# A looping load queue with register rows, and three outputs moved off TensorE in the last macro tile but one of rot90

## The chip, the cores and the metric

The kernel runs on one core of one Trainium2 chip. The metric is the time of one execution on the device, in microseconds (us). One execution per version is also taken with the hardware profiler; its trace gives the views used here.

## The reference

`x` is 8192 x 8192, float32. The kernel computes

```python
def reference(x, k):          # k = 1
    return np.rot90(x, k)
```

so `out[i, j] = x[j, 8191 - i]`: 268 MB are read, 268 MB are written, and nothing is calculated. Every 128x128 block has to be transposed on the way.

## The kernel before

**Tiles.** The input is cut into 16 macro tiles of 1024 rows x 4096 columns (numbered `kk`, 0 to 15). A macro tile is loaded in eight loads of 128 rows (2 MB each, row block `t`) and leaves in eight outputs (2 MB each, `j`), every output being 512 input columns of all 1024 rows. Load number `m` is `kk * 8 + t`, output number `n` is `kk * 8 + j`.

**Memory.** Loads land in two buffers in turn (`LAND = 2`; the first loads also use others). VectorE (DVE) takes each landed load and puts it, with its columns reversed, into the `ring`, which holds one macro tile less one chunk. An output is assembled in one of three buffers (`OUTS = 3`, chosen by the list `TURN`, L38) and stored from there. At the very end the landing buffers serve as output buffers too. Load `m` takes the ring places that output `m - 8` leaves, so DVE can only turn load `m` once output `m - 8` has been read out of the ring.

**Two ways to transpose.** `by_pe` (L196) says which outputs TensorE makes: all eight of tiles 0 and 15, outputs 0 and 4 of tiles 1 to 13, and outputs 0, 2, 4, 6, 7 of tile 14. For these DVE copies the load's columns into the ring (COPY), TensorE transposes 32 blocks of 128x128 against the identity into PSUM (`ps`), and ScalarE (ACT) evicts them into the output buffer. For all other outputs ("moved" ones) DVE transposes 32x32 squares on the way into the ring (STREAM_TRANSPOSE), and the squares then only need to be copied to their places in the output buffer: 16 copies of 32 partitions x 1024 elements, of which DVE makes 3, GpSimd (POOL) 8 and ACT 5 (`BY_DVE`, `BY_POOL`). One corner chunk of each tile has no place in the ring and goes through TensorE in any case; that is why output 7 has copies of 896 elements.

**Order of the work around the change.** Each engine has one program in order, and they meet in semaphores:

- SyncE (SP) issues nearly all loads (`by_sync`, L446, from load 5 on; `load_in_turn`, L400); ACT issues loads 1, 3 and 5 and halves of loads 6 to 9. Load `m` waits until DVE has turned the load that was in its buffer before (`taken`, L307).
- DVE (`by_vector`, L450), for load `m`: makes its 3 copies of output `n = m - 8` if that one is moved (after `room_for`, L295, has seen the store out of its buffer landed), waits for the load, waits until POOL and its own copies of output `n` are through (or TensorE has read it), and then turns load `m` into the ring, in the pieces that `by_pe` and the reach of one instruction give.
- POOL (`by_gpsimd`, L421) makes its 8 copies of each moved output; the eighth waits for ACT's five.
- ACT (`by_scalar`, L539) goes through the outputs in order: evictions for TensorE's, five copies for moved ones, and then it issues the store. For a moved output it waits first until DVE's first piece of load `n + 8` is done, which stands for POOL and DVE being through.
- TensorE (`by_tensor`, L493) transposes its outputs in order, in two PSUM halves.

**Loops.** An engine's program is recorded first (`Program`, L109) and then played. Two macro tiles make one turn of a loop on the engine (`loop`, L136); wait values are worked out from the loop register. In the kernel before, POOL loops over tiles 1 to 12, DVE and TensorE over tiles 2 to 13, in 6 turns each; SP and ACT are written out in full. All played instructions are issued on one line, L104, so the profile tells them apart by their tiles. SP's loads, which are not played, stand on L391.

The lines that decide who makes what, and the loops:

```python
    def by_pe(kk):
        if kk in (0, KK - 1):
            return list(range(J))
        return BY_PE if kk < KK - 2 else [*range(0, J, 2), J - 1]
```

Of the kernel before, what the change touches and what calls it, by code (L numbers as in the profile page):

```python
# [6 lines left out]
P = 128  # L7
# [3 lines left out]
T = R // P  # L11
W = 4096
# [48 lines left out]
class Place:  # L61


    def __init__(self, out, top, rows, left, cols):
        self.out, self.top, self.rows, self.left, self.cols = out, top, rows, left, cols
# [8 lines left out]
        return (self.top, self.rows, self.cols)  # L74


def key_of(v):
    if isinstance(v, bass.AP):
        return (v.tensor.name, v.offset, str(list(v.ap)))
    if isinstance(v, Place):  # L80
        return v.key()
    return str(v)


class Op:
# [13 lines left out]
    def run(self, e, shift=0, value=None):  # L99
        if self.name == "wait_ge":  # L100
            e.wait_ge(self.args[0], self.args[1] if value is None else value)  # L101
            return
        kwargs = {k: v.at(shift) if isinstance(v, Place) else v for k, v in self.kwargs.items()}
        i = getattr(e, self.name)(*self.args, **kwargs)  # L104
        if self.inc:
            i.then_inc(*self.inc)


class Program:  # L109
# [26 lines left out]
    def loop(self, nc, e, first, times):  # L136
        turns = [
            [op for kk in (first + 2 * i, first + 2 * i + 1) for op in self.parts[kk]]
            for i in range(times)
        ]  # L140
        for i, ops in enumerate(turns):
            assert len(ops) == len(turns[0]), (str(e.engine), i, len(ops), len(turns[0]))
            for a, b in zip(ops, turns[0]):
                assert a.key() == b.key(), (str(e.engine), i, a.key(), b.key())
        with nc.Fori(1, times + 1, engines=[e.engine]) as i:  # L145
            passed = nc.alloc_semaphore("passed") if e is nc.gpsimd else None
            waited = False
            for ops in zip(*turns):
                op = ops[0]
                if waited and op.name != "wait_ge" and passed is not None:  # L150
                    e.sem_inc(passed, 1)  # L151
                waited = op.name == "wait_ge"
                if op.name == "wait_ge":
                    n = [o.args[1] for o in ops]
                    step = n[1] - n[0]
                    assert n == [n[0] + k * step for k in range(times)]
                    assert n[0] > 0 and step >= 0
                    op.run(e, value=i * step + (n[0] - step) if step else n[0])
                    continue
                left = [v.left for o in ops for v in o.kwargs.values() if isinstance(v, Place)]  # L160
                if left:
                    step = left[1] - left[0]
                    assert left == [left[0] + k * step for k in range(times)]
                    op.run(e, shift=i * step - step)
                else:
                    op.run(e)
# [7 lines left out]
def kernel(tc: tile.TileContext, x: bass.AP, k: bass.AP, out: bass.AP):  # L174
# [21 lines left out]
    def by_pe(kk):  # L196
        if kk in (0, KK - 1):
            return list(range(J))
        return BY_PE if kk < KK - 2 else [*range(0, J, 2), J - 1]

    def in_quadrants(kk, j):
        return j not in by_pe(kk)
# [145 lines left out]
    def at(v, first, dims):  # L348
        return bass.AP(
            tensor=v.tensor, offset=v[:, first : first + 1].offset, ap=[v.ap[0], *dims]  # L350
        )
# [32 lines left out]
    def load(e, m, queue):  # L384
        r0, c0 = macros[m // T]
        b = load_buf(m)
        rows = slice(0, P)
        if m in BOTH:
            rows = slice(0 if queue is nc.sync else 1, P, 2)
        r = r0 + m % T * P  # L390
        e.dma_start(  # L391
            out=bufs[b][rows, :], in_=x[r : r + P, c0 : c0 + W][rows, :]
        ).then_inc(s_land[b], 16)

    def queues(m):
# [4 lines left out]
    def load_in_turn(e, m, queue):  # L400
        if queue not in queues(m):
            return
        last = [i for i in range(m) if load_buf(i) == load_buf(m)]
        taken(e.wait_ge, last[-1])
        load(e, m, queue)
# [4 lines left out]
    def turned_in(n):  # L410
        kk, _, (j,), _ = outs[n]
        return rev[kk * T + T - 1 - (j == J - 1), j]

    with tc.tile_critical():
        for m in range(LAND + OUTS):
            for e in queues(m):
                load(e, m, e)
    tc.close()
    tc.compile()  # L419

# [24 lines left out]

    def by_sync(e):  # L446
        for m in range(LAND + OUTS, n_load):
            load_in_turn(e, m, nc.sync)

    def by_vector(e):  # L450
        wait = once(e)
        for m in range(n_load):
            kk, t = divmod(m, T)
            e.part(kk)
            b = load_buf(m)
            n = m - T
            if n >= 0 and moved[n]:
                room_for(wait, n)
                wait(s_rev, turned_in(n))
                for to, of in moves(n, pairs[:BY_DVE]):  # L460
                    i = e.tensor_copy(out=to, in_=of)
                i.then_inc(s_dve, 1)
            e.wait_ge(s_land[b], landings(m))
            if n >= 0:
                if moved[n]:
                    e.wait_ge(s_pool, moved_until(n))
                    e.wait_ge(s_dve, moved_until(n))
                else:
                    e.wait_ge(s_half, turned_until(n))
            for js in pieces[m]:  # L470
                if (m, js[0]) == (n_load - 1, J - 1):
                    e.wait_ge(s_half, turned_until(KK * J - J))
                if kk < KK - 1 and (t, js[0]) == (T - 1, J - 1):
                    wait(s_rev, rev[m, 0])
                    e.tensor_copy(
                        out=at(bufs[b][:], 0, [[CH, 1], [1, CH]]), in_=landed(b, js)
                    ).then_inc(s_rev, 1)
                    continue
                turn = e.transpose if in_quadrants(kk, js[0]) else e.tensor_copy
                turn(out=chunk(kk, t, js), in_=landed(b, js)).then_inc(s_rev, 1)  # L480
# [12 lines left out]
    def by_tensor(e):  # L493
        e.part(-1)
        wait = once(e)
        e.wait_ge(s_id, 2)
        used = {}
        for n, some in in_turn():
            kk, ts, js, blocks = outs[n]
            e.part(kk)  # L500
            rows = len(ts) * P
            order = [(part, f) for part in some for f in part[2]]
            if js[0] == 0 and kk < KK - 1:
                late = parts[n][-1]
                order.sort(key=lambda o: (o[0] == late, o[1] % rows, o[1]))
            last = dict(order)
            for part, f in order:
                _, h, cols = part
                j, off = blocks[f // rows]
                t = ts[f % rows // P]  # L510
                if kk < KK - 1 and js[0] == 0 and f == parts[n][-1][2][0]:
                    m = kk * T + T - 1
                    wait(s_rev, rev[m, J - 1])
                    wait(s_freed, kk)
                    for g in range(G):
                        i = e.transpose(
                            corner[:, g * P : g * P + P],
                            bufs[load_buf(m)][:, g * P : g * P + P],
                            ident,
                        )  # L520
                    i.then_inc(s_corner, 1)
                if n == KK * J - J and h:
                    wait(s_freed, KK - 1)
                if used.get(h, part) != part:
                    wait(s_ev, evicted[used[h][0]] + 1)
                wait(s_rev, rev[kk * T + t, j])
                if part == parts[n][0] and f == last[part] and n != FIRST[1] and not tight(n):
                    room_for(wait, n)
                to = cols.index(f) * P
                i = e.transpose(  # L530
                    ps[h][:, to : to + P],
                    chunk(kk, t, [j])[:, 0, off : off + P],
                    ident,
                )
                if f == last[part]:
                    i.then_inc(s_half, 1)
                    used[h] = part
# [46 lines left out]
                in_=bufs[b][:, : groups * rows].rearrange("m (g f) -> m g f", f=rows),  # L584
            ).then_inc(s_store[b], 16)

    by_sync(nc.sync)
    for e, by, first, times in (
        (nc.gpsimd, by_gpsimd, 1, 6),
        (nc.vector, by_vector, 2, 6),  # L590
        (nc.tensor, by_tensor, 2, 6),
        (nc.scalar, by_scalar, None, 0),
    ):
        program = Program()
        by(program)
        program.play(nc, e, first, times)
# [39 lines left out]
```

## Time and profile before

| | |
|---|---|
| time, median of 3 runs | 1258.96 us (1258.8 to 1259.03) |
| the profiled execution: its own time | 1259.08 us |
| the profiled execution: span from first to last instruction | 1257.8 us |
| HBM read and written | 268.44 MB and 268.44 MB, 427 GB/s over the span |
| busy share of the span: PE, DVE, ACT, POOL | 24%, 63%, 48%, 59% |
| instructions | 6012 |
| loads | 124 of 2 MB and 8 halves of 1 MB; 125 of them issued by SP, 7 by ACT |
| stores | 128 of 2 MB, all issued by ACT |

How to read it: the span is cut into 40 slices of about 31 us for the rows of busy tenths; the DMA row there is the mean busy share of the core's 16 DMA engines, and the GB/s row what they moved. A timeline row has the start in us from the beginning of the span, the duration, the engine, the line, the operation, the tiles written and read, the shapes, and how many instructions were merged; in square brackets stands the idle time before it and what ended it. `ACTq` is ScalarE's sequencer, which issues DMAs. The chain of waits is the chain of work that ended last, in order of time. The packet records are the single DMA transfers in the trace: each 2 MB load or store is 128 packets of 16 KB, eight on each of the 16 DMA engines, and loads and stores have a queue each.

### The profile page before, as it was taken

What the parts mean: (1) busy time and instruction counts of PE and PEld (TensorE: products, weight loads), DVE (VectorE), ACT (ScalarE), POOL (GpSimd) and SP (SyncE); (2) the same over time, 40 slices, a digit from 0 to 9 for tenths busy, and PEclk for the clock granted to TensorE, in tenths of its full rate; (3) what the DMA queues carried; (4) which work ended last, traced back from release to release, by engine and by line L of the source; (5) the groups of instructions that cost most, each with busy time, mean ns of one, the idle gap of its engine ahead of it and who ended that gap; (6) DMA issues with size and microseconds to landing.
All of it is one profiled execution on the core that took longest, in us unless ns stands there. A gap on an engine that the chain in (4) does not pass through costs nothing.

```text
span 1257.8 us, 6012 instructions
## 1 busy us (share of the span) xinstructions
PE 302.9 (24%) x1556; PEld 264.8 (21%) x1556; DVE 793.8 (63%) x535; ACT 599.6 (48%) x556; POOL 744.0 (59%) x654
## 2 busy tenths in 40 slices
PE   1555013130131301313022130221302213024273
PEld 0454012130121301212012120121202212024273
DVE  2544866668666676666867667676677766764410
ACT  0334364463644636446364453645535455355364
POOL 0001966668666686666956668576685766965500
PEclk9987556555555555555556555565555556555597
DMA  9999999999999999999999999999999999999999
GB/s 400 420 430 429 429 429 429 429 431 430 430 430 429 430 428 430 428 430 430 430 430 429 431 428 431 428 430 428 430 430 429 430 429 431 427 423 428 427 428 381
DMA packets 36946, 537.09 MB, mean 427 GB/s; under 512 B 4160, under 2 KB 4160, under 8 KB 4160
## 3 DMA queue, kind: packets, MB, share of 16 engines
q10 hardware_dynamic: 19184, 278.93, 52.2%
q1 hardware_dynamic: 17744, 257.96, 48.0%
q8 instruction: 7, 0.11, 0.0%
q14 instruction: 11, 0.09, 0.0%
HBM read 268.44 MB, written 268.44 MB: 427 GB/s over the span
## 4 chain that ended last, share of the span: by engine, by line
DMA 71%; DVE 14%; ACT 4%; POOL 4%; issue 3%; PE 2%; ACTq 0%; DVEq 0%; SPq 0%; POOLq 0%
DMA buf<-in_x_dram 57%; DMA out_dram<-buf 14%; DVE ring L104 14%; ACT buf L104 4%; POOL buf L104 4%; PE ps L104 2%; ACTq L104 0%; DVE buf L104 0%; DVEq L101 0%; SPq L391 0%; DVEq L145 0%; POOLq L101 0%; SPq L311 0%; POOLq L151 0%; SPq L419 0%
## 5 line engine op out<-in xcount | busy, mean ns | idle before, releaser
L104 POOL COPY buf<-ring 32x1024 f32<-32x1024 f32 (+1 forms) x648 | 743.3, 1147 | 440.4 <-DMA out_dram<-buf 244.2
L104 ACT COPY buf<-ring 32x1024 f32<-32x1024 f32 (+1 forms) x405 | 414.8, 1024 | 324.2 <-DVE ring L104 292.5
L104 PE MATMUL ps<-head,ring 128*128 128x128 f32 x1496 | 290.7, 372 | 889.4 <-ACT buf L104 535.8
L104 PEld LDWEIGHTS ps<-head,ring 128*128 128x128 f32 x1496 | 255.3, 197 | 921.5 <-ACT buf L104 548.7
L104 DVE COPY ring<-buf 128x1024 f32<-128x1024 f32 (+5 forms) x152 | 157.7, 1044 | 415.6 <-DMA buf<-in_x_dram 320.1
L104 DVE STREAM_TRANSPOSE ring<-buf 128x3072 f32<-128x3072 f32 (+2 forms) x125 | 358.0, 2872 | 0.0
L104 ACT COPY buf<-ps 128x2048 f32<-128x2048 f32 (+4 forms) x149 | 183.3, 1278 | 313.6 <-DMA out_dram<-buf 149.3
L104 DVE COPY buf<-ring 32x1024 f32<-32x1024 f32 (+1 forms) x243 | 289.5, 1192 | 2.2
L104 PE MATMUL ps<-head,buf 128*128 128x128 f32 x60 | 15.2, 401 | 46.3 <-DVE buf L104 46.3
L104 PEld LDWEIGHTS ps<-head,buf 128*128 128x128 f32 x60 | 9.7, 199 | 52.0 <-issue 44.6
L104 DVE COPY buf<-buf 128x512 f32<-128x512 f32 x15 | 5.8, 387 | 0.0
L104 ACT ACT_TABLE_LOAD x1 | 1.3, 1283 | 3.4 <-PEq L419 3.4
L104 POOL MEMSET head<- 128x128 f32 x1 | 0.2, 204 | 2.9 <-POOLq L419 2.9
L104 POOL TENSOR_SCALAR_AFFINE_SELECT head<-head 128x128 f32<-128x128 f32 x1 | 0.3, 293 | 0.2 <-POOL head L104 0.2
L617 POOL MEMSET const-float32-0.0<- 128x1 f32 x1 | 0.1, 98 | 0.2 <-issue 0.2
L104 ACT COPY head<-head 128x1 f32<-128x1 f32 x1 | 0.2, 191 | 0.0
L617 POOL MEMSET const-bfloat16-1.0<- 128x1 bf16 x1 | 0.1, 100 | 0.0
L617 POOL MEMSET const-uint8-127<- 128x1 uint8 x1 | 0.1, 100 | 0.0
L617 POOL MEMSET const-float32-1.0<- 128x1 f32 x1 | 0.1, 98 | 0.0
## 6 DMA issues: line engine op xcount, KB each, us to landing
out_dram<-buf ACTq DMA_DIRECT2D x128, 2048.0 KB, 15.8
buf<-in_x_dram SPq DMA_DIRECT2D x121, 2048.0 KB, 15.0
buf<-in_x_dram ACTq DMA_DIRECT2D x3, 2048.0 KB, 16.9
buf<-in_x_dram SPq DMA_DIRECT2D x4, 1024.0 KB, 16.1
buf<-in_x_dram ACTq DMA_DIRECT2D x4, 1024.0 KB, 16.4
```

The lines of the kernel that those rows point to most:

```text
L104: i = getattr(e, self.name)(*self.args, **kwargs)
L617: nc = _bacc.Bacc("TRN2", target_bir_lowering=False, num_devices=1)
```

## The change

Four things change.

1. SP's program is recorded and played like the others: loads of tiles 2 to 13 are issued in a loop of 6 turns. The input rows are given by a new class `Rows`, which adds the loop register to the first row. In the loop each wait stands as an instruction of its own in front of the load and also counts up a semaphore; behind it come two small register instructions (the wait's value, the address) for every load. The destination and the length of the loads are unchanged, 128 rows of 4096 columns.
2. `by_pe` gives tile 14 the outputs 0 and 4 like tiles 1 to 13. Outputs 2, 6 and 7 of tile 14 become moved ones: 24 copies more on POOL, 15 on ACT in place of its evictions, 9 on DVE; and DVE turns the loads of tile 14 with one smaller COPY and one larger STREAM_TRANSPOSE each.
3. TensorE loops over tiles 1 to 14 and POOL over tiles 1 to 14, in 7 turns; TensorE starts its list of waits anew at tile 1, so that the turns are alike.
4. DVE waits, before its copies of a moved output, for the turn of the last of the tile's moved outputs instead of that output's own; at that point it has already gone through all of the tile's loads itself.

```diff
+class Rows:
+    def __init__(self, x, top, few, cols):
+        self.x, self.left, self.few, self.cols = x, top, few, cols
+
+    def at(self, shift):
+        if isinstance(shift, int):
+            return self.x[self.left + shift : self.left + shift + P, self.cols][self.few, :]
+        return self.x[bass.ds(self.left + shift, P), self.cols]
...
         with nc.Fori(1, times + 1, engines=[e.engine]) as i:
-            passed = nc.alloc_semaphore("passed") if e is nc.gpsimd else None
+            passed = None
+            if e in (nc.gpsimd, nc.sync):
+                passed = nc.alloc_semaphore(f"passed_{e.engine}")
...
                     op.run(e, value=i * step + (n[0] - step) if step else n[0])
+                    if e is nc.sync:
+                        e.sem_inc(passed, 1)
+                        waited = False
                     continue
...
     def by_pe(kk):
         if kk in (0, KK - 1):
             return list(range(J))
-        return BY_PE if kk < KK - 2 else [*range(0, J, 2), J - 1]
+        return BY_PE
...
         e.dma_start(
-            out=bufs[b][rows, :], in_=x[r : r + P, c0 : c0 + W][rows, :]
+            out=bufs[b][rows, :], in_=Rows(x, r, rows, slice(c0, c0 + W))
         ).then_inc(s_land[b], 16)
...
     def by_sync(e):
         for m in range(LAND + OUTS, n_load):
+            e.part(m // T)
             load_in_turn(e, m, nc.sync)
...
-                wait(s_rev, turned_in(n))
+                wait(s_rev, max(turned_in(i) for i in range(n - n % J, n - n % J + J) if moved[i]))
...
             e.part(kk)
+            if n == J:
+                wait = once(e)
...
-    by_sync(nc.sync)
     for e, by, first, times in (
-        (nc.gpsimd, by_gpsimd, 1, 6),
+        (nc.sync, by_sync, 2, 6),
+        (nc.gpsimd, by_gpsimd, 1, 7),
         (nc.vector, by_vector, 2, 6),
-        (nc.tensor, by_tensor, 2, 6),
+        (nc.tensor, by_tensor, 1, 7),
         (nc.scalar, by_scalar, None, 0),
```

More of the change, by code (lines that the diff above doesn't have):

```diff
@@ L74, in key @@
         return (self.top, self.rows, self.cols)
+class Rows:
[5 more added lines that the diff above has]
+        return self.x[bass.ds(self.left + shift, P), self.cols]
+    def key(self):
+        return (str(self.few), str(self.cols))
+MOVED = (Place, Rows)
 def key_of(v):
@@ L79, in key_of @@
         return (v.tensor.name, v.offset, str(list(v.ap)))
-    if isinstance(v, Place):
+    if isinstance(v, MOVED):
         return v.key()
@@ L102, in run @@
             return
-        kwargs = {k: v.at(shift) if isinstance(v, Place) else v for k, v in self.kwargs.items()}
+        kwargs = {k: v.at(shift) if isinstance(v, MOVED) else v for k, v in self.kwargs.items()}
         i = getattr(e, self.name)(*self.args, **kwargs)
@@ L158, in loop @@
                     op.run(e, value=i * step + (n[0] - step) if step else n[0])
+                    if e is nc.sync:
+                        e.sem_inc(passed, 1)
+                        waited = False
                     continue
-                left = [v.left for o in ops for v in o.kwargs.values() if isinstance(v, Place)]
+                left = [v.left for o in ops for v in o.kwargs.values() if isinstance(v, MOVED)]
                 if left:
@@ L416 @@
             for e in queues(m):
-                load(e, m, e)
+                program = Program()
+                program.part(0)
+                load(program, m, e)
+                program.play(nc, e)
     tc.close()
```

## The prediction

> Names: output kk.j is output j of macro tile kk, load kk.t its row block t. "Steady" is the stretch from about 700 to 1058 us.
>
> **What bounds the kernel now.** I read the page's slices of the span first, then the busy times by stretch, then the timeline of POOL, DVE and ACT in the last 120 us, then the packet records of the two data queues.
>
> The DMA engines are full from 40 us to 1240 us, at 430 GB/s in the steady part:
>
> ```profile
> DMA  9999999999999999999999999999999999999999
> GB/s 400 420 430 429 429 429 429 429 431 430 430 430 429 430 428 430 428 430 430 430 430 429 431 428 431 428 430 428 430 430 429 430 429 431 427 423 428 427 428 381
> ```
>
> Four stretches: a steady tile, then the outputs of tile 13, of tile 14, and of tile 15 with the end (after the comma: busy us of PE, PEld, DVE, ACT, POOL, then clock, DMA share, GB/s):
>
> ```profile
> 918.00:996.00 78.00, 14.77 (x68) 12.95 (x68) 55.98 (x38) 38.56 (x37) 54.04 (x49) 0.52 1.01 430
> ...
> 1058.56:1135.47 76.91, 14.20 (x68) 12.46 (x68) 53.37 (x43) 38.69 (x37) 60.04 (x48) 0.54 1.01 426
> 1135.47:1211.01 75.54, 32.97 (x172) 28.93 (x172) 30.02 (x18) 34.48 (x31) 32.90 (x24) 0.60 1.01 428
> 1211.00:1257.80 46.80, 24.38 (x208) 22.49 (x208) 0.59 (x2) 25.45 (x14) 0.00 (x0) 0.85 0.93 396
> ```
>
> Nothing is lost to waiting except in the last row (and the first 40 us). So an edit costs time only where both data queues run empty together. One load and one store, 4.19 MB, take 9.76 us at 430 GB/s: that is the period that compute has to keep.
>
> POOL is closest to it. Its eight copies of one output, in a steady tile and in tile 14, where DVE turns loads of tile 15 with one plain copy:
>
> ```profile
> 981.64 9.29 POOL L104 COPY buf<-ring 32x1024 f32<-32x1024 f32 x8 [8.92 <-DMA out_dram<-buf]
> ```
> ```profile
> 1138.11 11.63 POOL L104 COPY buf<-ring 32x1024 f32<-32x1024 f32 x8 [8.21 <-DMA out_dram<-buf]
> 1140.53 2.90 DVE L104 COPY ring<-buf 128x4096 f32<-128x4096 f32 x1 [6.29 <-DMA buf<-in_x_dram]
> ...
> 1150.31 2.29 DVE L104 COPY ring<-buf 128x4096 f32<-128x4096 f32 x1 [2.54 <-DMA buf<-in_x_dram]
> ```
>
> Of those eight, the one under DVE's 128x4096 copy took 3.00 us (1141.33), the three under DVE's 32x1024 copies 1.40 each, the rest 1.03. The stores of the end:
>
> ```profile
> 1191.77 0.55 ACTq L104 DMA_DIRECT2D out_dram<-buf  x1
> 1192.36 3.70 ACT L104 COPY buf<-ps 128x2048 f32<-128x2048 f32 x3 [5.61 <-DVE ring L104]
> 1196.09 0.55 ACTq L104 DMA_DIRECT2D out_dram<-buf  x1
> ```
>
> 14.5 (POOL's) is issued at 1191.77 and 14.6 (TensorE's) only 4.3 us later. 14.7 follows at 1203.07, 15.0 at 1211.01, the rest every 4.26 us. By the packet records the last load is through at 1207.4; 14.7's packets begin at 1210.1 and 15.0's at 1215.0, 7.0 and 4.0 us after their issues. From an issue to its first packet on a queue that had run dry I find 2.1 us (store at 1094.06), 3.5 (load at 1096.91), 3.6 (store at 1024.26), 3.8 (store at 1152.63), and 1.05 at the kernel's start (0.91) with nothing else in flight. So 15.0 has about half a microsecond to spare today.
>
> **The change, part by part.** SyncE's loop: 96 of its loads get a register address and two small register instructions behind the wait; six turns add a branch. An engine that starts after a wait here does so in 0.45 to 0.5 us, register waits or not (POOL 981.64, ACT 1157.63), so I bound the delay by 0 and 0.5 us a load. DVE's own loop branch shows the other price: in the chain of waits a load lands at 426.51 and DVE's copy starts at 428.57, against 0.5 us elsewhere, so 1.5 us a turn. I take both at nothing: the store queue covers them. Near 1027 us the store queue is dry until 1027.9, the load queue from 1028.4 to 1031.1, the store queue again from 1036.8. A load would have to be over 5 us late before both are dry together. Without that cover it would be 6 x 1.5 = 9 us for the branches and at most 96 x 0.5 = 48 us for the loads.
>
> TensorE's and POOL's seventh turn, the reset of TensorE's list of waits, DVE's wait for a count that it has itself passed already: nothing. TensorE is busy 24% of the span.
>
> Loads of tile 14: DVE's turn goes from copies of 2048 and 512 columns and a transpose of 1536 (2.8 + 1.76 us) to a copy of 1024 and a transpose of 3072 (0.7 to 1.4, + 3.36), the steady form. POOL copies beside it fall back to 9.3 us an output (60.04 busy to 54.04 in the rows above). Tile 13 then runs as a steady tile: 14.0 goes out 78.2 us after 13.0, at 1136.8 instead of 1135.5, with the DMA full throughout. No gain in itself: an earlier 430 instead of 426 GB/s only empties the queues sooner if the stores behind are late.
>
> Tile 14: outputs 2, 6 and 7 leave TensorE (92 transposes) for the three copying engines: POOL gets 24 copies, ACT 15 in place of 9 evictions, DVE 9. The ACT (5.26 against 3.70) and the DVE part (three of 1.43) are hidden behind POOL's. POOL now has 14.1, 14.2, 14.3 in a row, then 14.5, 14.6, 14.7, all beside DVE's 128x4096 copies: 3.00 + 3 x 1.40 + 4 x 1.03 and the gaps are 11.6 us an output, against the period of 9.76.
>
> The chain, step by step. DVE starts the next load's copy 0.45 us after POOL ends (1091.86 to 1092.33); it takes 2.7 us (2.65 to 2.90 beside POOL), and its end releases the store and the next load together. A load and a store that start together need 9.8 us and land 1.3 us later. Latency 3.5 us at first:
> - 14.1: POOL to 1149.7 as before, store 1152.9.
> - 14.2: POOL to 1161.4, store 1164.6, and load 15.4 with it. All that was issued before is through at 1166.3, so the DMA idles to 1168.1.
> - 14.3: POOL to 1173.0, store and load 15.5 at 1176.2. Idle again, 1177.9 to 1179.7.
> - 14.4 (TensorE) needs 14.2's buffer: 1164.6 + 3.5 + 9.8 + 1.3 and 0.6 is 1179.9; + 3.7 is 1183.6.
> - 14.5: POOL's last copy waits for ACT's five, to 1189.5, and ends at 1190.6; load 15.5 lands at 1190.8; store 1194.1.
> - 14.6 needs 14.3's buffer, 1190.9: POOL 1191.4 to 1203.5, store 1206.6.
> - 14.7: 896 columns, 10.7 us: POOL to 1214.2, then 0.45 and DVE's first piece 0.44: store **1215.1, 12 us later** than now.
> - 15.0: ACT evicts only after that: 1220.7.
>
> By then only stores are left and the queue is dry. From 14.7 on there are nine stores, which now take 44.9 us (the slowest DMA engine's landings 1212.4 to 1257.3); 15.0 adds 0.6. End: 1215.1 + 3.5 + 44.9 + 0.6 = 1264.1, + 6.8. With 2.0 us of latency the buffers come 1.5 us sooner and 14.7 goes at 1213.6: end 1261.1, + 3.8. With 1.05 at every dry start, + 2.0. With 3.8, about + 7.5. I take the middle of 2.0 and 3.5, which the dry starts span: **+ 5.3 us**. The profiled execution took 1259.08 (span 1257.8), 0.1 above the median shown, so 1264.4, rounded to 1264.3.
>
> **The rivals.**
> *It is covered, about the same (0.20).* If the blocked copies do not add up, tile 14 runs with the steady spacing: in tile 12, output 7 goes out 72.3 us after output 0 and the next tile's 0 after 78.0. From 1136.8 that gives 14.7 at 1209.1; with 2.0 us of latency its packets start at 1211.1 instead of 1210.1: + 1.0, 1260.1 (1257.5 to 1261.4). For it: POOL has idled some 8 us before several outputs of this stretch. Against: in the new order that idle time lies only at 14.1, 14.5 and 14.6.
>
> *Faster (0.07).* One mechanism: fewer bytes and a cleaner stage in front of an end that holds. 426 to 430 GB/s over 77 us is 0.7 us. The slowest DMA engine ends 2.5 us after the mean of the sixteen, and TensorE's code comes in 16 KB packets of 0.95 to 1.03 us, each on one engine (1104.9, 1191.2, 1219.3, 1236.0 in the end part); 92 transposes less save one or two. Together at most 3.2: 1255.9. It decides only if 14.7 is issued by 1206.6 and 15.0 by 1211.5, where the queue is still fed. The Trainium skill (SBUF — State Buffer, Who interferes with whom) has it that DMA does not contend with a compute engine; by that the 0.7 us would not come from DVE's copies. The rows show 426 beside them and 430 without, which does not settle the cause.
>
> *The loops cost (0.05).* If SP's loop makes loads late by more than the 5 us of cover, at a branch above all, the six turns give 9 us: 1268 and more. Against it: DVE and POOL already loop, and from 210 to 1100 us the DMA view has 430 GB/s and seven instruction packets of 8 KB in all. The Trainium skill (Runtime: NRT & Kernel Launch, Instruction fetch mechanics) warns that a taken branch out of the two pages held forces a fetch and a stall. By that rule each turn would fetch; seven packets for some 17 turns of three engines do not look like it.
>
> **How the numbers follow.** Forecast 0.68, at 1264.3, its own span 1261.1 (latency 1.05) to 1267 (3.8). The rivals 0.20, 0.07, 0.05. About 0.2%, 2.5 us, is what a measurement of this kernel can tell from no change. Range 1259.5 to 1268.0: it leaves out the faster case, most of the loop case and the lower half of the covered one. Slower 0.68 + 0.05 = 0.73; same 0.20; faster 0.07.
>
> **What would show it.** Right: POOL at 11 to 12 us an output from 1138 us on, 14.2's store near 1164, 14.7's near 1213 to 1215, a DMA share clearly below 1 between 1205 and 1220, the steady rows unchanged at 430 GB/s. Wrong: 14.7 before 1209, a DMA share of 1 up to 1240, or a rate below 429 in the middle, which would be SP's loop. The weakest step is the latency of a dry queue, next the assumption that every blocked copy costs its full 3.00 us.

## The result, and the profile after

| | before | after |
|---|---|---|
| time, median | 1258.88 us (1258.55 to 1259.03, 6 runs) | 1265.04 us (1263.76 to 1265.93, 6 runs) |
| ratio | | **1.0048**, 95% interval 1.0037 to 1.0058 |
| profiled execution: time, span | 1259.08, 1257.8 us | 1264.82, 1263.5 us |
| instructions | 6012 | 6324 |

The change made the kernel 0.48% slower. The forecast was 1264.3. The page's row of GB/s shows where the 5.7 us of span came from:

```profile
GB/s 398 422 430 428 428 431 430 429 428 431 430 430 428 429 431 430 429 429 429 431 429 429 428 432 431 429 428 430 431 431 429 428 431 431 430 413 415 403 382 393
```

The loop's long stretch is at 430 as before. The slices from 1105 us on, which had 423 to 428, are now 413, 415, 403 and 382; the first of these is still tile 13, the others cover tile 14 and the start of tile 15. The same by stretch, after: a steady tile, the outputs of tile 13, of tile 14, of tile 15 (columns as in the prediction):

```profile
918.00:996.00 78.00, 14.41 (x68) 12.57 (x68) 51.52 (x38) 38.72 (x38) 52.58 (x48) 0.57 1.01 430
1059.14:1137.36 78.22, 14.57 (x68) 12.74 (x68) 53.42 (x37) 38.78 (x37) 52.73 (x48) 0.54 1.01 423
1137.36:1220.67 83.31, 16.19 (x80) 15.03 (x80) 44.87 (x28) 38.78 (x37) 65.82 (x48) 0.55 0.97 401
1220.67:1263.50 42.83, 24.39 (x208) 22.49 (x208) 0.00 (x0) 25.45 (x14) 0.00 (x0) 0.89 0.93 393
```

Tile 14 takes 83.3 us instead of 75.5, POOL's busy time in it doubles from 32.9 to 65.8, and the rate is 401. Tile 13's stretch, at 423 instead of 426, makes some 0.5 us. The rest of the loss lies in two places of tile 14's stretch, which three windows separate, first before, then after:

```profile
1150.00:1190.00 40.00, 15.30 (x69) 13.10 (x67) 16.94 (x11) 17.81 (x16) 21.57 (x16) 0.54 1.01 428
1190.00:1210.00 20.00, 11.69 (x80) 10.49 (x80) 4.88 (x4) 10.87 (x9) 0.00 (x0) 0.76 1.01 428
1210.00:1225.00 15.00, 12.71 (x111) 11.65 (x110) 1.59 (x2) 12.08 (x8) 0.00 (x0) 1.00 1.01 427
```
```profile
1150.00:1190.00 40.00, 1.11 (x4) 0.71 (x4) 22.32 (x13) 19.31 (x18) 32.45 (x24) 0.50 0.98 395
1190.00:1210.00 20.00, 2.40 (x11) 2.40 (x12) 13.41 (x8) 9.13 (x10) 19.18 (x14) 0.50 1.01 431
1210.00:1225.00 15.00, 11.27 (x70) 10.46 (x69) 2.52 (x3) 8.76 (x7) 2.77 (x3) 0.79 0.78 328
```

In the middle (1150 to 1190) 33 of 428 GB/s over 40 us are 3.1 us of DMA work not done; at the end (1210 to 1225) 99 of 427 over 15 us are 3.5. The two places are not alike. By the packet records the engines are idle for all of the 3.5 us at the end, but for only 0.8 of the 3.1 us in the middle; there some 2.3 us are load packets that take longer (see the last section). About 0.9 us comes back: in the last stretch the mean DMA engine now ends 1.6 us before the slowest, and 2.5 in the kernel before.

The timeline of POOL, DVE and ACT shows the chain behind both:

```profile
1138.24 44.49 POOL L122 COPY buf<-ring 32x1024 f32<-32x1024 f32 x31 [8.57 <-DMA out_dram<-buf]
...
1161.64 3.15 DVE L122 COPY ring<-buf 128x4096 f32<-128x4096 f32 x1 [3.13 <-POOL buf L122]
...
1164.82 0.55 ACTq L122 DMA_DIRECT2D out_dram<-buf  x1
...
1173.32 3.16 DVE L122 COPY ring<-buf 128x4096 f32<-128x4096 f32 x1 [4.21 <-POOL buf L122]
1176.51 0.55 ACTq L122 DMA_DIRECT2D out_dram<-buf  x1
```

POOL works 44.5 us without a pause, and DVE's copies of loads 15.2 and 15.3, which had waited for DMA, wait for POOL. POOL's single copies in the chain of waits are as forecast:

```profile
1152.09 2.99 POOL buf L122
1155.11 1.40 POOL buf L122
1156.56 1.40 POOL buf L122
1158.00 1.40 POOL buf L122
1159.44 0.66 POOL buf L122
1160.52 1.03 POOL buf L122
```

The first is the one under DVE's 128x4096 copy, the next three lie under DVE's copies of 32x1024, the rest is alone (the chain cuts the 0.66). And the end, on ACT:

```profile
1213.44 0.55 ACTq L122 DMA_DIRECT2D out_dram<-buf  x1
1214.03 3.21 ACT L122 COPY buf<-ps 128x2048 f32<-128x2048 f32 x2 [2.68 <-PE ps L122]
1220.05 0.58 ACT L122 COPY buf<-ps 128x512 f32<-128x512 f32 x1 [2.82 <-PE ps L122]
1220.67 0.55 ACTq L122 DMA_DIRECT2D out_dram<-buf  x1
```

14.7 is stored at 1213.44, 15.0 at 1220.67. By the packet records all but one of 14.6's packets are through at 1213.8 (that one at 1214.4), 14.7's run from 1214.65 to 1219.7, 15.0's begin at 1221.9. So the store queue, by then the only one, is empty for about 1 us and then for 2.2 us.

### The profile page after: what moved, and what is told of

It reads as the page before. It is cut to its first block, busy times and chain, and to the rows that moved or that the text cites. A ratio compares the mean times of both kernels' runs of the same rounds, so it can differ in the third digit from the quotient of the medians.

```text
span 1263.5 us, 6324 instructions
## 1 busy us (share of the span) xinstructions
PE 290.3 (23%) x1464; PEld 254.7 (20%) x1464; DVE 774.9 (61%) x538; ACT 604.0 (48%) x562; POOL 756.9 (60%) x678
## 4 chain that ended last, share of the span: by engine, by line
DMA 69%; DVE 14%; POOL 5%; issue 4%; ACT 3%; PE 1%; ACTq 0%; SPq 0%; DVEq 0%; POOLq 0%
DMA buf<-in_x_dram 60%; DVE ring L122 14%; DMA out_dram<-buf 9%; POOL buf L122 5%; ACT buf L122 3%; PE ps L122 1%; ACTq L122 0%; SPq L122 0%; DVEq L119 0%; DVE buf L122 0%; SPq L180 0%; POOLq L119 0%; DVEq L163 0%; POOLq L171 0%; POOLq L163 0%
## 5 line engine op out<-in xcount | busy, mean ns | idle before, releaser
L122 POOL COPY buf<-ring 32x1024 f32<-32x1024 f32 (+1 forms) x672 | 756.2, 1125 | 452.5 <-DMA out_dram<-buf 233.0
L122 ACT COPY buf<-ring 32x1024 f32<-32x1024 f32 (+1 forms) x420 | 429.9, 1024 | 353.8 <-DVE ring L122 329.2
L122 PE MATMUL ps<-head,ring 128*128 128x128 f32 x1404 | 276.9, 376 | 902.7 <-ACT buf L122 565.5
L122 PEld LDWEIGHTS ps<-head,ring 128*128 128x128 f32 x1404 | 244.5, 199 | 932.1 <-ACT buf L122 571.0
L122 DVE COPY ring<-buf 128x1024 f32<-128x1024 f32 (+2 forms) x145 | 144.8, 1001 | 442.5 <-DMA buf<-in_x_dram 378.9
L122 DVE STREAM_TRANSPOSE ring<-buf 128x3072 f32<-128x3072 f32 (+2 forms) x126 | 370.2, 2947 | 0.0
L122 ACT COPY buf<-ps 128x2048 f32<-128x2048 f32 (+3 forms) x140 | 172.6, 1279 | 289.5 <-DMA out_dram<-buf 136.2
L122 DVE COPY buf<-ring 32x1024 f32<-32x1024 f32 (+1 forms) x252 | 271.5, 1078 | 2.3
## 6 DMA issues: line engine op xcount, KB each, us to landing
out_dram<-buf ACTq DMA_DIRECT2D x128, 2048.0 KB, 15.2
```

## The experiments

Theory A: all of the loss is tile 14; late outputs let both queues run empty, part in the middle and part at the end. Rival B: SP's loop takes part of it. Rival C: only the end counts. Later rivals stand with their runs. In the table "not moved" is DMA time worked out like the 3.1 and 3.5 us above (against 428 and 427 GB/s); "longer" is the median against the kernel before in the same runs. The rates are those of one profiled execution each, which can lie over 1 us from the median (e5's took 1262.98 us, e7's 1260.66), so the two columns agree only roughly.

| kernel | 1150-1190 | 1210-1225 | not moved, us | longer, us | ratio, 95% interval |
|---|---|---|---|---|---|
| after | 395 | 328 | 3.1 + 3.5 | 6.2 | 1.0048 (1.0037 to 1.0058) |
| e1_loops_only | 426 | 425 | 0.2 + 0.1 | 0.4 | 1.0004 (0.9995 to 1.0013) |
| e2_tile14_only | 401 | 336 | 2.5 + 3.2 | 4.9 | 1.0044 (1.003 to 1.0058) |
| e3_out2_moved | 399 | 428 | 2.7 + 0 | 1.9 | 1.0014 (1.0005 to 1.0023) |
| e4_out67_moved | 431 | 340 | 0 + 3.1 | 2.5 | 1.0019 (1.001 to 1.0028) |
| e5_out7_moved | 428 | 323 | 0 + 3.7 | 2.9 | 1.0025 (1.0016 to 1.0034) |
| e6_pool_two_fewer | 414 | 369 | 1.3 + 2.0 | 2.1 | 1.0013 (1.0004 to 1.0022) |
| e7_early_store | 412 | 360 | 1.5 + 2.4 | 2.8 | 1.0022 (1.0013 to 1.0031) |
| e8_loops_early_store | 430 | 426 | 0 + 0 | -0.1 | 1.0002 (0.9993 to 1.0011) |
| e9_evict_ahead | 395 | 385 | 3.1 + 1.5 | 3.6 | 1.0027 (1.0016 to 1.0037) |
| e10_both | 414 | 410 | 1.3 + 0.6 | 0.5 | 1.0004 (0.9995 to 1.0013) |

**Which part of the change: e1 and e2.** e1 is the changed kernel with the old choice for tile 14 (and POOL and TensorE in 6 turns, since tile 14 differs again):

```diff
-        return BY_PE
+        return BY_PE if kk < KK - 2 else [0, 2, 4, 6, 7]
```

> The changed kernel with tile 14 as it was (TensorE makes 0, 2, 4, 6, 7), so only the loops and the register rows are left. Theory A (the whole loss is tile 14, where POOL's outputs are late and the DMA queues run dry): the 0.22 us that SP's loads are later in the loop (0.25 us after DVE's end instead of 0.03) stay hidden, 1258.9 us as the kernel before, within 0.5. Rival B (part of the loss is the loop, 96 x 0.22 = 21 us of lateness partly uncovered): 1260 to 1263, with the rate below 429 GB/s between 210 and 1000 us.

Measured: 1259.25 us against 1258.83. The loop cost nothing that these runs can tell (by the interval at most 1.6 us), and its long stretch is at 430 GB/s:

```profile
210.00:1000.00 790.00, 148.55 (x680) 130.54 (x680) 526.22 (x375) 392.41 (x375) 536.46 (x486) 0.55 1.01 430
```

e2 is the kernel before with `return BY_PE` and nothing else.

> The kernel before with only outputs 2, 6 and 7 of tile 14 moved off TensorE, SP written out in full, loops of 6 turns. Theory A: the full loss, 1265 us (1264 to 1266), 14.7 stored near 1213 us and 15.0 near 1220. Rival B: 1261 to 1263, the rest of the loss being the loop's.

Measured: 1263.77 us, 0.2 under theory A's range and 0.8 above rival B's; 14.7 stored at 1212.18, 15.0 at 1218.74. With e1, rival B falls as far as these runs can tell: tile 14 alone has a ratio of 1.0044, and its interval holds that of the whole change.

**Middle or end: e3, e4, e5.** Each is e1 with another list for tile 14: `[0, 4, 6, 7]`, `[0, 2, 4]`, `[0, 2, 4, 6]`.

> Of tile 14 only output 2 is moved (TensorE makes 0, 4, 6, 7). Theory A: the first half of the chain alone, POOL making 14.1, 14.2, 14.3 in a row at 11.6 us: 14.2 stored near 1164.8 and 14.3 near 1176.5, the rate down to some 400 GB/s between 1150 and 1190, which is 2.5 to 3 us lost for good since the end stays fed by TensorE's 14.6 and 14.7: 1261.5 us (1260.7 to 1262.5). Rival C (only the end counts, a hole in the middle is made up later because the stores have reserve there): 1258.9.

Measured: 1260.72 us, 14.2 stored at 1164.0 and 14.3 at 1175.7. The rate is 399 in the middle and 428 at the end; in e4, below, it is the other way round (first e3, then e4):

```profile
1150.00:1190.00 40.00, 4.58 (x19) 3.78 (x19) 22.39 (x14) 19.32 (x18) 32.03 (x24) 0.50 1.00 399
1210.00:1225.00 15.00, 12.43 (x107) 11.36 (x106) 1.74 (x2) 11.49 (x7) 0.00 (x0) 1.00 1.01 428
```
```profile
1150.00:1190.00 40.00, 7.43 (x37) 6.21 (x36) 16.87 (x11) 17.81 (x16) 24.01 (x19) 0.59 1.01 431
1210.00:1225.00 15.00, 10.45 (x77) 9.70 (x78) 2.34 (x3) 10.29 (x7) 0.00 (x0) 0.89 0.80 340
```

ACT in e3 shows the pace at which POOL and DVE release its stores:

```profile
1153.42 0.55 ACTq L122 DMA_DIRECT2D out_dram<-buf  x1
1154.00 5.25 ACT L122 COPY buf<-ring 32x1024 f32<-32x1024 f32 x5 [11.11 <-DVE ring L122]
1164.03 0.55 ACTq L122 DMA_DIRECT2D out_dram<-buf  x1
1164.62 5.25 ACT L122 COPY buf<-ring 32x1024 f32<-32x1024 f32 x5 [5.37 <-DVE ring L122]
1175.71 0.55 ACTq L122 DMA_DIRECT2D out_dram<-buf  x1
```

10.6 and 11.7 us between stores, where the DMA needs 9.76. Rival C falls: a loss in the middle is mostly not made up, though the end has stores in reserve. Of the 2.7 us not moved, 0.8 came back. But theory A's picture of empty queues does not fit the middle: the DMA share there is 1.00, the engines are idle for 0.3 us, and nearly all of the 2.7 us are load packets that take longer. That the late stores bring this about is shown by e3 against e4 and e8; how they do is not.

> Of tile 14 outputs 6 and 7 are moved (TensorE makes 0, 2, 4). Theory A: no hole before 1200 us; 14.6 stored near 1202.7, 14.7 near 1211, 15.0 near 1218, the queue dry twice for some 2 us each, about 1.3 of it given back because the slowest DMA engine catches up: 1262 us (1261 to 1263.5). Rival C: the full 1265, as the end is all that counts.

Measured: 1261.3 us; 14.6 at 1202.27, 14.7 at 1210.28, 15.0 at 1217.24. As theory A had it. e3 and e4 together (1.9 + 2.5) make most of the 4.9 of e2.

> Of tile 14 only output 7 is moved (TensorE makes 0, 2, 4, 6). POOL then has two periods for it and no backlog. Theory A1 (at the end a moved output is late in itself: it starts when 14.4's buffer is free, near 1197, takes POOL 10.7 us, and ACT can evict 15.0 only behind it): 14.7 stored near 1209.5, 15.0 near 1216.7, one dry hole: 1260 to 1261. Rival A2 (the lateness is POOL's backlog from three moved outputs in a row): 1259.

Measured: 1261.85 us, and A2 falls: the store times are those of A1 (1209.30, 1216.99), but the price was too low. One moved output at the very end costs as much as two. There are two holes, not one, since 15.1 is late as well. ACT in e5:

```profile
1209.30 0.55 ACTq L122 DMA_DIRECT2D out_dram<-buf  x1
1209.89 3.21 ACT L122 COPY buf<-ps 128x2048 f32<-128x2048 f32 x2 [7.99 <-DVE ring L122]
1216.37 0.59 ACT L122 COPY buf<-ps 128x512 f32<-128x512 f32 x1 [3.28 <-PE ps L122]
1216.99 0.55 ACTq L122 DMA_DIRECT2D out_dram<-buf  x1
```

ACT idles 8 us in front of 14.7's store, and only behind it evicts 15.0, the first 28 of whose transposes TensorE had done by 1204.2.

**Is it POOL's pace: e6, e7, e8.** e6 leaves two of POOL's eight copies out in tile 14:

```diff
+                    if kk == KK - 2 and c in (1, 2):
+                        continue
```

> The changed kernel with two of POOL's eight copies left out for each moved output of tile 14 (those blocks of the output are not written anew), POOL in 6 turns. Theory A (POOL's 11.6 us an output against 9.76 is what makes 14.2 and 14.3 late): 8.5 us an output; 14.3 stored near 1173.7 instead of 1176.5, 14.7 near 1209.3 instead of 1213.4: 1261 (1260.3 to 1262). Rival D (the store's wait for DVE's whole turn and ACT's order set the pace): 1264 and more.

Measured: 1261.09 us; 14.3 at 1173.94, 14.7 at 1209.80. Both stand where POOL's pace puts them, so rival D falls as the only cause. e7 keeps POOL's work and turns each load of tile 15 but the last in two pieces, so that ACT's store waits for the first 1024 columns alone:

```diff
-            got = [here] if t < T - 1 else [here[:wide], here[wide:-1], here[-1:]]
+            got = [here[:2], here[2:]] if t < T - 1 else [here[:wide], here[wide:-1], here[-1:]]
```

> The changed kernel with tile 15's loads turned in two pieces (1024 columns, then 3072), so that a moved output of tile 14 is stored some 2 us sooner, while POOL's work stays. Theory A: the two holes between 1150 and 1190 shrink, 14.2 and 14.3 stored near 1162.5 and 1174, but POOL's chain to 14.7 keeps its pace: 1263 to 1264. Rival D: the whole loss goes, 1259 to 1260.

Measured: 1261.8 us, between the two. The middle went as theory A had it (14.2 at 1161.8, 14.3 at 1173.3). The end gained more than I had allowed: 14.3's store lands at 1187.0 instead of 1190.5, so POOL starts 14.6 sooner, and 14.7 goes at 1209.6 instead of 1213.4. I had taken POOL's chain there as fixed, but it starts from a store's landing.

e8 is e1 with the edit of e7.

> The kernel of e1 (loops and register rows, tile 14 as before) with the early store of e7. Theory A: no queue runs dry there, so an earlier store is worth nothing: 1259 within 0.6. Rival D: under 1258.

Measured: 1258.89 us. The stores are up to 2.6 us sooner (14.3 at 1170.85 instead of 1173.50), and it is worth nothing, because the two queues together are at 430 GB/s there (426 in e1) as it is.

**Can it be closed: e9, e10.** In e9 ACT evicts 15.0's first half before it waits to store 14.7 (the eviction became a function `evict`):

```diff
                 i.then_inc(s_act, 1)
+                if n + 1 == FIRST[0]:
+                    room_for(wait, n + 1)
+                    evict(n + 1, parts[n + 1][:1])
                 e.wait_ge(s_rev, rev[n + T, pieces[n + T][0][0]])
```

> The changed kernel, but ACT evicts the first PSUM half of 15.0 before it waits to store 14.7, instead of after. Theory A1 (the last hole comes from ACT's order: 15.0 goes out 7.2 us after 14.7, while a store alone takes 4.9): 14.7 still stored near 1213.4, 15.0 near 1216.8 instead of 1220.7, the hole after 14.7 closed: 1262.5 (1261.5 to 1263.5). Rival A3 (14.7's own lateness is the whole price at the end): 1265.

Measured: 1262.47 us. A3 falls. ACT in e9:

```profile
1211.01 1.87 ACT L122 COPY buf<-ps 128x2048 f32<-128x2048 f32 x1
1213.09 0.55 ACTq L122 DMA_DIRECT2D out_dram<-buf  x1
1213.68 1.44 ACT L122 COPY buf<-ps 128x1536 f32<-128x1536 f32 x1 [0.80 <-DVE ring L122]
1215.86 0.59 ACT L122 COPY buf<-ps 128x512 f32<-128x512 f32 x1 [0.74 <-PE ps L122]
1216.48 0.55 ACTq L122 DMA_DIRECT2D out_dram<-buf  x1
```

The half is evicted in the idle time, 14.7 is no later, and 15.0 follows after 3.4 us instead of 7.2. e10 has the edits of e7 and e9 together.

> e9 and the early store of e7 together: holes in the middle mostly closed, 14.7 near 1209.6, 15.0 near 1213, no hole after it. Theory A: 1260 to 1260.8, within 0.2% of the kernel before, though TensorE makes two outputs of tile 14. Rival A3: 1261.8 as e7.

Measured: 1259.41 us, better than theory A's 1260. ACT in e10, the stores of 14.7 and 15.0:

```profile
1210.23 0.55 ACTq L122 DMA_DIRECT2D out_dram<-buf  x1
...
1213.62 0.55 ACTq L122 DMA_DIRECT2D out_dram<-buf  x1
```

With the two delays taken off, the change's division of the work is level with the kernel before; it does not beat it, and neither does any other kernel tried. For most of the span both are held by the DMA, at 430 GB/s in the steady tiles.

## Why the prediction was right

**SyncE's loop, taken at nothing because the store queue covers it: right.** Loads in the loop are issued 0.25 us after DVE's end instead of 0.03; the two that wait for the corner 1.12 and 1.17 instead of 0.99. So it is 0.22 us a load and nothing visible for the branch, against my bounds of 0.5 and 1.5. The 96 x 0.22 = 21 us vanish (e1). The Trainium skill's warning (Runtime: NRT & Kernel Launch, Instruction fetch mechanics) is of a taken branch whose target lies outside the two pages held, so "each turn would fetch" in the prediction read more into it than it says. No fetch at each turn shows in the traces: between 210 and 1100 us there are four instruction packets of 8 KB after the change, with its added loop, and seven before, and none of 16 KB in either.

**POOL at 11.6 us an output: right**, by the copies shown above. The steps of the chain, forecast (the case with 3.5 us of latency) and measured:

| store | 14.0 | 14.1 | 14.2 | 14.3 | 14.4 | 14.5 | 14.6 | 14.7 | 15.0 |
|---|---|---|---|---|---|---|---|---|---|
| before | 1135.5 | 1152.6 | 1157.0 | 1172.6 | 1180.9 | 1191.8 | 1196.1 | 1203.1 | 1211.0 |
| forecast | 1136.8 | 1152.9 | 1164.6 | 1176.2 | 1183.6 | 1194.1 | 1206.6 | 1215.1 | 1220.7 |
| after | 1137.4 | 1154.2 | 1164.8 | 1176.5 | 1183.3 | 1192.8 | 1205.4 | 1213.4 | 1220.7 |

**The sum, + 5.3 forecast, + 5.7 in the span: right, by errors that cancel.** The latency of 14.7's dry queue was taken between 2.0 and 3.5 us; it was 1.2 (issue 1213.44, first packet 1214.65), and the same for 15.0 (1220.67 to 1221.88). 14.7's issue came a little before both of the prediction's cases (1213.6 and 1215.1). So the hole before 14.7 was about 1 us, less than forecast. But the hole behind it, which I had at 0.6, was 2.2: 15.0 went out 7.2 us after 14.7 and not 5.6, since ACT waited 2.82 us more for TensorE before the last piece of 15.0. And the nine stores without that hole took 46.2 us to the last packet (1214.65 to 1263.04) instead of 44.9. Two terms were too large and two too small; that the total fits to 0.4 us, and 15.0's issue to the tenth, is luck. 15.0's issue, set by ACT's order, held the end in any case, as e9 shows.

**The idle stretches in the middle: right in place** (forecast 1166.3 to 1168.1 and 1177.9 to 1179.7). The lowest rates lie there: in the records the mean number of packets under way falls to 14.0 in the microsecond from 1167 and to 9.8 in that from 1177, from 16.1. But the mechanism is only part of it. The prediction had two idle stretches of 1.8 us each; the engines were idle for 0.8 us in all, and 2.3 of the 3.1 us are load packets that took longer, which the prediction did not have. So its rule that time is lost only where both queues run empty together held at the end and not in the middle.

**The cleaner stage of tile 13, worth 0.7 us in the rival "faster": not seen here, and not settled.** With POOL back at 52.7 busy us the rate there was 423, not 430. But over nearly the same stretch (1058 to 1136 us) other kernels with the new stage had 429 (e2, e6) and 430 (e7), and two with the old one 424 (e1) and 429 (e8). So the rate differs as much between traces of the same stage as between the stages, and DVE's copies alone do not set it. What goes with a low rate is again longer packets: 49 packets of over 0.7 us between 1120 and 1138 us in the changed kernel, none in e2 and e7. Why they come stays open.

The rivals "covered" and "loops" fell with e2 to e5 and e1.

## What to carry to other kernels

Where the DMA is full nearly throughout, lateness costs nothing as long as the two queues together keep up the rate: in e8 stores up to 2.6 us sooner were worth nothing. Where the stores of tile 14 came too late it cost time that was mostly not made up (1.9 of 2.7 us in e3), at the end as idle engines and in the middle mostly as slower load packets. So look for the places where reserve is thin, here the passage to the last tile, and price a moved piece of work there by its engine's time under the contention of that stage (11.6 us, not the steady 9.3) against the period (9.76). An engine that works in order can also hold back what comes behind its wait; moving one eviction ahead of such a wait was worth 2.6 us (e9).

## What the runs showed of the hardware

- A queue that starts with nothing else in flight has its first packet 1.2 us after the issue (twice in the changed kernel). In the kernel before, with the other queue busy, it was 2.1 to 3.8. A busy second queue alone is not the reason: in e7 the store of 14.3, issued at 1173.28, has its first packets at 1174.50, 1.2 us later, with 11 to 15 load packets under way. What sets the difference is not settled.
- A full DMA share is not a full rate. Between 1150 and 1190 us the share is 0.98 and the rate 395; in e3 the share is 1.00 and the rate 399. Of the 527 load packets that start there in the changed kernel 61 take over 0.8 us, up to 1.8, where the median is 0.611; in the kernel before 5 of 535 do. Together the longer packets make some 2.3 us, spread over the 16 engines, and idle engines 0.8. Most of them start while the store queue is nearly empty or has just been. That alone is not enough either: at 1027 us in the kernel before the loads were nearly alone too, and took 0.61. Why these packets take longer is not settled.
- A load whose address comes from a register, in a loop with its wait apart, is issued 0.22 us later than one written out (0.25 instead of 0.03 us after DVE's end).
